# Ten more channel pairs by seven products, with three of a pair's four weight sums made ahead in place of two

## The chip, the cores and the metric

The kernel runs on one core of one Trainium2 chip, in one launch. The metric is the device time of one execution in microseconds (us), lower is better. The core's engines are TensorE (PE, with its weight loads as PEld), VectorE (DVE), ScalarE (ACT), GpSimd (POOL) and SyncE (SP, which here issues DMAs).

## The reference

A decoder trunk of two layers on 256 tokens of width 2048, all in float32. Layer 0 is a Mamba-2 mixer, layer 1 a MoBA cross-attention whose keys and values come from the stream after layer 0. Each is followed by a gated MLP with a causal convolution of width 3. Every sub-layer ends in `h = layer_norm(4**0.25 * h + f(h))`.

```
mix = mamba2_mixer(h, ...)             # ... -> y @ w_out          (4096 x 2048)
ffn = (silu(gate) * val) @ w_down      # gate, val: conv(h @ w_up) (5632 x 2048)
k_blk, v_blk, k_mean = shared_kv(h, w_kv)
mix = moba_cross_attention(h, w_q, w_o, k_blk, v_blk, k_mean)
```

What matters here are the products of the tokens with large weight matrices: `w_out`, the two `w_down`, the third of the V columns and `w_o`. All of them read each weight once.

## The kernel before, in words

A float32 product is made of three faster ones: each operand x is split into a rounded part hi (type fp32r) and a rest lo, and the product is hi*hi + hi*lo + lo*hi. The weights come in tiles `raw` of 128 x 2 x 512 (512 KB) from `in_w`, which the host has stacked in the order of use. `split` makes hi on ACT (L357) and lo on DVE (L358), up to `LA` + 1 = 4 tiles ahead of PE, in a ring of `RING` = 5 pairs of buffers; the `raw` tiles have `RAW` = 4 buffers. A tile is loaded when the one four before it has been read.

The work is one list of **steps**, a tile each; for every step the program runs what is hung before it (`pre`), its matmuls (`products`), amid which later tiles are split, and what is hung after it (`post`, by `at(i, f)`). So the order on every engine follows from the step's number, and DMAs, sums and normalizations are placed by step numbers.

Most products are ordinary. The "duos" (class `Duo`) take two neighbouring blocks of 512 columns, a and b, with the two halves of the tokens, and the channels in **pairs** of two blocks of 128. A pair is either two ordinary steps (kind `a` or `b`, twelve matmuls of 512 columns each, in `half`: L392, L393, L396) or goes **by seven products** (a form of Strassen's: seven of 128 x 128 x 512 in place of eight), as two steps `A` and `B`: two products, six matmuls, in A, and five products, fifteen matmuls, in B (`one`: L413, L414, L415). The seven need four sums of the pair's activations, and four of its four weight blocks W11, W22 (tile A), W21, W12 (tile B): W11+W12, W22+W12, W11+W12+W22 and all four. `SUMS` writes, for each matrix, the order of the steps of both its duos: `a`, `b`, and `H` for a pair by seven products whose weight sums are begun ahead.

**Weight sums ahead.** For an `H`, `plan_hoist` makes W11+W12 and W22+W12 stages earlier and keeps them in DRAM (`made`): with `away`, by a DMA that copies and one of POOL's that accumulates (L645, L648; for mamba's output and the V projection); else by loads into a tile `hoist` and a half tile `u`, one add on DVE (L661) and a store (L664). The list `starts` says at which steps; the three parts of one lie at s, s + 4 and s + 6. When the pair is due, `load` fetches for the B step W21 into `raw` (L287) and both sums into `gb` (L288; `mA` in mamba's stage), and `split_sums` adds on DVE the third (L327, which reads tile A once more) and the fourth (L328), and splits W21 (`u`, L320 and L325), the first two (L326, L329) and the last two (L330, L331).

**Activation sums.** They are made when the activations are (`make_sums`: four subtractions L597 to L600, a cast, a subtraction L607, a store to DRAM) and fetched by POOL (`fetch_sums`, L622) into eight ring slots in `hT`, each slot again when the pair that used it is done. POOL works its queue in order.

**Normalization.** The end of each duo adds its banks to the residual on DVE (`Norm.sums`, `add2`), at steps counted from the last pair by seven products; the residual tiles `r` are loaded at the start of each duo.

Of the kernel before, what the change touches and what calls it, by code (L numbers as in the profile page):

```python
# [18 lines left out]
F32 = mybir.dt.float32  # L19
F32R = mybir.dt.float32r  # L20
AF = mybir.ActivationFunctionType
OP = mybir.AluOpType
AX = mybir.AxisListType

P = 128
# [14 lines left out]
NC = 512  # L40
# [6 lines left out]
for _name, _n in (("cw", 4 * CONV), ("cb", CONV), ("nw", DI), ("fw0", 6 * DFF), ("fcb0", 2 * DFF), ("fw1", 6 * DFF),  # L47
# [10 lines left out]
SIZE = 2 * PIECE  # L58
AT = 16
RING = LA + 2  # L60
SUMS = {"mamba": ("aabbababab" + "HabHaHbHabH", "aaHaHabHaHabHaH"), "att": ("aabbHaHbHbaab", ""), "v": ("aHHaHHbHabb",),
        0: ("aabbaba" + "HaHb" * 5 + "Hbbaab", "aaHaHbHaHaHbHaHbHaHaHb"), 1: ("aabbaba" + "HaHb" * 5 + "Hbbaab", "aaHaHbHaHaHbHaHbHaHaHb")}
SLOTS = 8


# [3 lines left out]

MOST = {n: max(map(count, SUMS[k])) for n, k in ((DI, "mamba"), (D, "att"), (DFF, 0))}  # L70
INTO = {"a": ("P2", "p4"), "b": ("p3", "N22"), "A": ("P1", "p3"), "B": ("P2", "p5", "P7", "p6", "p4")}
# [3 lines left out]
def chunks():  # L75
# [71 lines left out]
def yoco_kernel(ctx: ExitStack, tc: tile.TileContext, x, lmg, lmb, lfg, lfb, x_t, columns, w, out):  # L147
    nc = tc.nc
    base = ctx.enter_context(tc.tile_pool(name="base", bufs=1))
    wts = ctx.enter_context(tc.tile_pool(name="wts", bufs=LA + 1))  # L150
    t4 = ctx.enter_context(tc.tile_pool(name="t4", bufs=4))
    psum = ctx.enter_context(tc.tile_pool(name="psum", bufs=1, space=bass.MemoryType.PSUM))
    dram = ctx.enter_context(tc.tile_pool(name="dram", bufs=1, space=bass.MemoryType.DRAM))
# [124 lines left out]
    def load():  # L278
        i = pos["load"]
        if i >= n_steps:  # L280
            return
        pos["load"] += 1
        raw_t[i] = t = wts.tile([P, 2, NC], F32, tag="raw", name="raw", bufs=RAW)
        if early(i):
            ch, s = steps[i]
            made_t[i] = y = ch.tmp()
            nc.sync.dma_start(t[:, 0], w[i][:, 0])  # L287
            nc.sync.dma_start(y, ch.sum_d[ch.items[s][1]])  # L288
            return
        for e in (slice(0, 1), slice(1, 2)) if i == 0 else (slice(0, 2),):  # L290
            nc.sync.dma_start(t[:, e], w[i][:, e])

    def early(i):
        return kind(i) == "B" and steps[i][0].items[steps[i][1]][1] in steps[i][0].sum_d
# [19 lines left out]
    def split_sums(i):  # L314

        ra, rb = raw_t.pop(i - 1), raw_t.pop(i)
        (yh, yl), (zh, zl) = (map(plain, ring_tiles()) for _ in range(2))
        wh, wl = (base.tile([P, 2, S], F32R, tag="u", name="u", bufs=2).rearrange("p k t -> p (k t)")
                  for _ in range(2))
        nc.scalar.copy(wh, rb[:, 0])  # L320
        yf, zf = (made_t.pop(i), rb) if early(i) else (steps[i][0].tmp() for _ in range(2))
        t2, t4 = (zf[:, k] for k in ((1, 0) if early(i) else (0, 1)))
        if not early(i):
            nc.vector.tensor_add(yf, ra, rb[:, 1:2, :].to_broadcast([P, 2, NC]))
        nc.vector.tensor_sub(wl, rb[:, 0], wh.bitcast(F32))  # L325
        nc.scalar.copy(yh, yf)  # L326
        nc.vector.tensor_add(t2, yf[:, 0], ra[:, 1])  # L327
        nc.vector.tensor_add(t4, t2, rb[:, 0])  # L328
        nc.vector.tensor_sub(yl, yf, yh.bitcast(F32))  # L329
        nc.scalar.copy(zh, zf)  # L330
        nc.vector.tensor_sub(zl, zf, zh.bitcast(F32))  # L331
        hi_t[i], lo_t[i] = [wh, yh, zh], [wl, yl, zl]
        load()
        load()
# [68 lines left out]
    def one(i, b, unit, h, l):  # L403
        ch, s = steps[i]
        p = ch.items[s][1]
        if isinstance(unit, int):
            u = sum_units(ch.sums, ch.slot[p])
            xh, xl = u[:, 0, unit], u[:, 1, unit]
        else:
            kk, t = unit  # L410
            xh, xl = (f(2 * p + kk)[:, t * P:(t + 1) * P] for f in (ch.x.hi, ch.x.lo))
        a, begins, ends = ch.into(b, i)
        nc.tensor.matmul(a, xh, h, start=begins, stop=False)  # L413
        nc.tensor.matmul(a, xh, l, start=False, stop=False)  # L414
        nc.tensor.matmul(a, xl, h, start=False, stop=ends)  # L415

    def duo_products(i):
        ch, s = steps[i]
        ch.use(i)
        name, p = ch.items[s]  # L420
        h, l = hi_t[i], lo_t[i]
        if name == "A":
            one(i, "P1", (0, 0), h[:, 0], l[:, 0])
            one(i, "p3", 3, h[:, 1], l[:, 1])
            run(mid, i)
            done(i)
            return splits(i)
        if name == "B":
            (wh, yh, zh), (wl, yl, zl) = h, l
            one(i, "P2", (1, 0), wh, wl)  # L430
            one(i, "p5", 0, yh[:, 0], yl[:, 0])
            one(i, "P7", 2, yh[:, 1], yl[:, 1])
            run(mid, i)
            t2, t4 = (1, 0) if early(i) else (0, 1)
            one(i, "p6", 1, zh[:, t2], zl[:, t2])
            one(i, "p4", (1, 1), zh[:, t4], zl[:, t4])
            done(i)
            return splits(i)
        side = ch.sides[name]
        ends = side.tail and i >= side.at[-side.tail]  # L440
        if side.tail and i == side.at[-side.tail]:
            side.piece = [(tp_tile() if side.tail == LAST else ch.bank[b][0])[:, :HC] for b in ("P1", "P7")]
        half(i, 0)
        if ends:
            if i < side.last:
                return splits(i)
            for q in range(2):
                for j in side.at[-side.tail:]:
                    half(j, 1, q)
                    if q:  # L450
                        done(j)
            return
        run(mid, i)
        splits(i)
        half(i, 1)
        done(i)
# [72 lines left out]
    def at(i, f, *a):  # L529
        post.setdefault(i, []).append((f, a))  # L530
# [103 lines left out]
    def plan_hoist(duo, starts, away=False):  # L634

        todo = [(du, p) for du in duo for p in du.early]
        assert len(starts) >= len(todo)
        for (du, p), s in zip(todo, starts):
            du.sum_d[p] = made = dram.tile([P, 2, NC], F32, name=f"made{du.first}_{p}")
            n = du.items.index(("A", p)) + du.first  # L640
            tiles = []
            if away:

                def copy(n=n, made=made):
                    nc.sync.dma_start(made, w[n])  # L645

                def more(n=n, made=made):
                    nc.gpsimd.dma_start(made, w[n + 1][:, 1:2].to_broadcast([P, 2, NC]), accum_op=OP.add)  # L648

                at(s, copy)  # L650
                at(s + 6, more)
                continue

            def fetch(n=n, tiles=tiles):
                tiles += [t4k("hoist"), base.tile([P, 2, S], F32, tag="u", name="u", bufs=2).rearrange("p k t -> p (k t)")]
                nc.sync.dma_start(tiles[0], w[n])
                nc.sync.dma_start(tiles[1], w[n + 1][:, 1])

            def add(tiles=tiles):
                y, b12 = tiles  # L660
                nc.vector.tensor_add(y, y, b12.unsqueeze(1).to_broadcast([P, 2, NC]))  # L661

            def store(made=made, tiles=tiles):
                nc.sync.dma_start(made, tiles[0])  # L664

            at(s, fetch)
            at(s + 4, add)
            at(s + 6, store)

# [148 lines left out]
    chX, chZ = [], []  # L818
# [19 lines left out]
    chO = duos("y", tmp_mamba)  # L838
    up0, down0 = ffn_chunks()
# [3 lines left out]
    chQ = []  # L843
# [6 lines left out]
    up1, down1 = ffn_chunks()  # L850
    n_steps = len(steps)
    for du in (chO, down0, chA, down1):
        plan_sums(du)
    plan_hoist(chO, [chX[0].first + 8 * k for k in range(12)], away=True)
    plan_hoist(down0, [up0[1][0].first + 7 * k for k in range(21)])
    plan_hoist([chW], [chV[0].first + 2 + 3 * k for k in range(5)], away=True)
    plan_hoist(chA, [chQ[0].first + 4 + 6 * k for k in range(3)])
    plan_hoist(down1, [chQ[0].first + 22 + 6 * k for k in range(4)] + [up1[1][0].first + 9 * k for k in range(17)])

    pool = {}  # L860

# [598 lines left out]
    for h in range(HEADS):  # L1460
        i, j = divmod(h, 4)
# [27 lines left out]
    def rest(h):  # L1489

        n3.center(0, h)
        n3.all_off(1, h)
        n3.store_half(1, h, eng=nc.scalar)
        n3.center(2, h)
        n3.scale(0, h)
        n3.store_half(0, h)
        n3.scale(2, h)
        n3.store_half(2, h)
        for q in range(2):
            n3.norm(3, h, slice(q * HC, (q + 1) * HC))  # L1500
# [55 lines left out]
```

## Time and profile before

| | |
|---|---|
| median of 3 runs | 2464.04 us (2461.68 to 2465.58) |
| span of the profiled execution, first to last instruction | 2461.0 us |
| PE busy | 2449.1 us, 17992 matmul records |
| DVE busy | 1897.3 us |
| ACT busy | 1390.5 us |
| POOL busy | 112.6 us |
| moved by DMA | 629.53 MB, 256 GB/s in the mean |
| mamba's output | about 483 to 650 us of the span |
| up, down of layer 0 | 682 to 1141, 1141 to 1365 us |
| K, V, Q and attention | about 1365 to 1740 us |
| up, down of layer 1 | 1767 to 2226, 2226 to 2453 us |

The profiled execution has no time of its own beside its span; the runs lie 0.7 to 4.6 us above it. A row of the timeline reads: start, duration, engine, line, operation, tiles written <- read, shapes, and in brackets the engine's idle time before it with what ended it. Matmuls overlap, so that a row's duration is longer than the distance to the next. In the rows of stretches the columns are: stretch, length, busy time (and count) of PE, PEld, DVE, ACT, POOL, the granted clock, the mean busy share of the 16 DMA engines, and GB/s.

### The profile page before, as it was taken

The page shows a single profiled execution, that of the slowest core. Times are in us where ns is not written, and L with a number is a line of the kernel's source. Part 1 is how long each engine was busy: PE and PEld are TensorE (multiplying, and loading weights), DVE is VectorE, ACT ScalarE, POOL GpSimd, SP SyncE. Part 2 cuts the span into 40 slices and gives each one's busy share as a digit, 9 for nine tenths or more (in the row PEclk, how much of TensorE's full clock was granted, in tenths as well). Part 3 has the DMA queues.
Part 4 walks back from the last instruction along what each step waited for, and adds up shares of the span by engine and source line. Part 5 has one row for each costly group of instructions (what it writes and reads, how often), then busy time and mean ns, then how long its engine had stood idle before and what let it go on. Part 6 is the DMA issues. An engine that isn't in the chain of part 4 may idle for free.

```text
span 2461.0 us, 44889 instructions
## 1 busy us (share of the span) xinstructions
PE 2449.1 (100%) x17992; PEld 2299.1 (93%) x17992; DVE 1897.3 (77%) x2533; ACT 1390.5 (57%) x1817; POOL 112.6 (5%) x147
## 2 busy tenths in 40 slices
PE   9999999999999999999999999999999999999998
PEld 9999999988899999999888889998899999998887
DVE  6768778878877777777898785768777677777997
ACT  6677677655455545545655464545555455455563
POOL 0010100100200000000000300000200000000001
PEclk9999999999999999999999999999999999999999
DMA  7677886767678787777878776768677778778775
GB/s 265 225 235 251 257 261 202 255 222 260 226 251 287 267 291 272 273 273 278 287 258 267 266 258 234 251 223 265 214 275 256 266 248 275 246 261 317 249 272 194
DMA packets 184753, 629.53 MB, mean 256 GB/s; under 512 B 20560, under 2 KB 21072, under 8 KB 184288
## 3 DMA queue, kind: packets, MB, share of 16 engines
q1 hardware_dynamic: 170032, 582.55, 68.8%
q0 software_dynamic: 14224, 43.59, 6.3%
q8 instruction: 141, 2.31, 0.4%
q14 instruction: 68, 0.56, 0.1%
q10 hardware_dynamic: 288, 0.52, 0.1%
HBM read 578.28 MB, written 65.08 MB: 261 GB/s over the span
## 4 chain that ended last, share of the span: by engine, by line
PE 98%; DVE 1%; ACT 0%; issue 0%; DMA 0%; SPq 0%; ACTq 0%
PE acc L489 62%; PE acc L392 7%; PE acc L396 7%; PE acc L393 7%; PE acc L415 3%; PE acc L413 3%; PE acc L414 3%; PE tp L415 1%; PE tp L413 1%; PE tp L414 1%; PE acc L1099 1%; PE tp L580 0%; PE tp L1108 0%; PE acc L1082 0%; PE tp L1402 0%; PE tp L1437 0%
## 5 line engine op out<-in xcount | busy, mean ns | idle before, releaser
L358 DVE TENSOR_TENSOR lo<-raw,hi 128x1024 fp32r<-128x1024 f32 (+1 forms) x808 | 973.0, 1223 | 256.8 <-ACT hi L357 254.9
L489 PE MATMUL acc<-hT,hi 128*128 128x256 f32 x8960 | 1116.1, 277 | 0.3 <-ACT hi L357 0.2
L489 PEld LDWEIGHTS acc<-hT,hi 128*128 128x128 f32 x8960 | 1061.6, 188 | 3.4 <-issue 1.2
L357 ACT CAST hi<-raw 128x1024 fp32r<-128x1024 f32 (+1 forms) x808 | 828.5, 1046 | 345.6 <-PE acc L489 138.1
L489 PE MATMUL acc<-hT,lo 128*128 128x256 f32 x4480 | 599.8, 276 | 0.0
L489 PEld LDWEIGHTS acc<-hT,lo 128*128 128x128 f32 x4480 | 550.1, 188 | 0.0
L937 DVE SCALAR_TENSOR_TENSOR v<-acc,cols,v 128x254 f32<-128x254 f32 (+1 forms) x176 | 72.7, 475 | 78.5 <-ACT v L932 78.4
L393 PE MATMUL acc<-lo,gT 128*128 128x512 f32 x334 | 129.4, 388 | 0.0
L392 PE MATMUL acc<-hi,gT 128*128 128x512 f32 x334 | 129.4, 388 | 0.0
L330 ACT CAST hi<-raw 128x1024 fp32r<-128x1024 f32 x61 | 64.3, 1055 | 87.1 <-DVE raw L328 86.5
L396 PE MATMUL acc<-hi,gT 128*128 128x512 f32 x334 | 102.5, 388 | 0.0
L932 ACT ACTIVATE v<-acc,cols 128x256 f32<-128x256 f32 x88 | 44.9, 561 | 93.8 <-PE acc L489 93.8
L622 POOL DMA_DIRECT2D hT<-sums x35 | 18.7, 539 | 1422.9 <-PE acc L489 949.4
L937 DVE SCALAR_TENSOR_TENSOR g<-acc,cols,g 128x255 f32<-128x255 f32 (+1 forms) x160 | 66.1, 475 | 19.5 <-ACT g L932 19.5
L1331 ACT CAST gT<-v 128x512 fp32r<-128x512 f32 x44 | 27.3, 621 | 93.0 <-DVE v L1330 93.0
L331 DVE TENSOR_TENSOR lo<-raw,hi 128x1024 fp32r<-128x1024 f32 x61 | 74.8, 1226 | 3.7
L393 PEld LDWEIGHTS acc<-lo,gT 128*128 128x128 f32 x334 | 62.7, 188 | 12.8
L392 PEld LDWEIGHTS acc<-hi,gT 128*128 128x128 f32 x334 | 62.7, 188 | 12.8
L396 PEld LDWEIGHTS acc<-hi,gT 128*128 128x128 f32 x334 | 62.6, 188 | 12.9
L932 ACT ACTIVATE g<-acc,cols 128x256 f32<-128x256 f32 x80 | 40.8, 560 | 42.0 <-PE acc L489 42.0
L326 ACT CAST hi<-gb 128x1024 fp32r<-128x1024 f32 x50 | 52.6, 1052 | 16.8 <-DMA gb<-made 14.6
L392 PE MATMUL acc<-hi,hT 128*128 128x512 f32 x152 | 61.9, 408 | 0.0
(332 smaller groups left out, 2946.8 us busy)
## 6 DMA issues: line engine op xcount, KB each, us to landing
raw<-in_w SPq DMA_DIRECT2D x819, 512.0 KB, 4.7
gb<-made SPq DMA_DIRECT2D x50, 512.0 KB, 5.2
hoist<-in_w SPq DMA_DIRECT2D x45, 512.0 KB, 6.4
made<-hoist SPq DMA_DIRECT2D x45, 512.0 KB, 6.2
hT<-sums POOLq DMA_DIRECT2D x35, 512.0 KB, 7.0
raw<-in_w SPq DMA_DIRECT2D x63, 256.0 KB, 3.8
sums<-st SPq DMA_DIRECT2D x31, 512.0 KB, 3.3
u<-in_w SPq DMA_DIRECT2D x45, 256.0 KB, 6.2
```

The source lines that it names most:

```text
L331: nc.vector.tensor_sub(zl, zf, zh.bitcast(F32))
L357: nc.scalar.copy(h[:, sl], t[:, sl])
L358: nc.vector.tensor_sub(l[:, sl], t[:, sl], h[:, sl].bitcast(F32))
L392: nc.tensor.matmul(a, th, h[:, kk, sl], start=begins and kk == 0, stop=False)
L393: nc.tensor.matmul(a, th, l[:, kk, sl], start=False, stop=False)
L396: nc.tensor.matmul(a, ch.x.lo(k)[:, ts], h[:, kk, sl], start=False, stop=ends and kk == 1)
L413: nc.tensor.matmul(a, xh, h, start=begins, stop=False)
L414: nc.tensor.matmul(a, xh, l, start=False, stop=False)
L415: nc.tensor.matmul(a, xl, h, start=False, stop=ends)
L489: nc.tensor.matmul(banks[j], w[:, a, n * P:(n + 1) * P], x(k0 + kk), start=k0 == 0 and j // 2 not in where[:at_n], stop=k0 + ch.per == ch. ...
L932: nc.scalar.activation(self.dst[:, self.jd + i, :], u[:, i % 2, :], AF.Identity, bias=c1(self.b, self.ia + i), scale=c1(self.at_w, w[n - 1 ...
L937: nc.vector.scalar_tensor_tensor(d, u[:, i % 2, :S - k], c1(self.at_w, w[n - 1 - k] + self.ia + i), d, op0=OP.mult, op1=OP.add)
```

## The change

1. `made` holds three sums in place of two: W11+W12, W11+W12+W22 and W22+W12. On DVE the one add of 1024 becomes three of 512; the store becomes two (512 and 256 KB). With `away`, the copy becomes two, the accumulation two of 256 KB, and a third accumulating DMA (s + 12) adds one row of sums to another, after the first two have landed.
2. For the B step `load` fetches a third piece, 256 KB of `made` into the second half of `raw`. `split_sums` adds only the fourth sum on DVE, and reads tile A no more. The last products of a B step come in another order, p6 before P7.
3. `SUMS`: mamba's output 6 and 7 pairs by seven products (before 5 and 6), each down projection 13 and 12 (before 11 and 10), often two pairs in a row.
4. The `starts` of `plan_hoist` are closer: 13 in place of 12 for mamba; 25 every 6 steps in place of 21 every 7 for down of layer 0; 4 and 21 every 7 in place of 4 and 17 every 9 for layer 1. More activation sums are made: 7 in place of 6 for mamba, 13 in place of 11 for each down projection.

```
-SUMS = {"mamba": ("aabbababab" + "HabHaHbHabH", "aaHaHabHaHabHaH"), ...
-        0: ("aabbaba" + "HaHb" * 5 + "Hbbaab", "aaHaHbHaHaHbHaHbHaHaHb"), 1: ...
+SUMS = {"mamba": ("aabbababab" + "HaHbHaHbHH", "aaHaHabHHaHbHaH"), ...
+        0: ("aabbab" + "HaHbHHaHHbHHaHbHHaHH" + "bbaab", "aaHaHHaHHbHaHHaHHaHHbaaa"), 1: ...
...
+            made = ch.sum_d[ch.items[s][1]]
             nc.sync.dma_start(t[:, 0], w[i][:, 0])
-            nc.sync.dma_start(y, ch.sum_d[ch.items[s][1]])
+            nc.sync.dma_start(y, made[:, :2])
+            nc.sync.dma_start(t[:, 1], made[:, 2])
...
-        nc.vector.tensor_add(t2, yf[:, 0], ra[:, 1])
-        nc.vector.tensor_add(t4, t2, rb[:, 0])
+        if made:
+            nc.vector.tensor_add(zf[:, 0], yf[:, 1], rb[:, 0])
+        else:
+            nc.vector.tensor_add(zf[:, 0], yf[:, 0], ra[:, 1])
+            nc.vector.tensor_add(zf[:, 1], zf[:, 0], rb[:, 0])
...
                 def copy(n=n, made=made):
-                    nc.sync.dma_start(made, w[n])
+                    nc.sync.dma_start(made[:, :2], w[n])
+                    nc.sync.dma_start(made[:, 2], w[n][:, 1])
                 def more(n=n, made=made):
-                    nc.gpsimd.dma_start(made, w[n + 1][:, 1:2].to_broadcast([P, 2, NC]), accum_op=OP.add)
+                    for k in (0, 2):
+                        nc.gpsimd.dma_start(made[:, k], w[n + 1][:, 1], accum_op=OP.add)
+                def rest(made=made):
+                    nc.gpsimd.dma_start(made[:, 1], made[:, 0], accum_op=OP.add)
                 at(s, copy)
                 at(s + 6, more)
+                at(s + 12, rest)
...
             def add(tiles=tiles):
                 y, b12 = tiles
-                nc.vector.tensor_add(y, y, b12.unsqueeze(1).to_broadcast([P, 2, NC]))
+                nc.vector.tensor_add(y[:, 0], y[:, 0], b12)
+                nc.vector.tensor_add(b12, b12, y[:, 1])
+                nc.vector.tensor_add(y[:, 1], y[:, 1], y[:, 0])
             def store(made=made, tiles=tiles):
-                nc.sync.dma_start(made, tiles[0])
+                nc.sync.dma_start(made[:, :2], tiles[0])
+                nc.sync.dma_start(made[:, 2], tiles[1])
...
-    plan_hoist(down0, [up0[1][0].first + 7 * k for k in range(21)])
+    plan_hoist(down0, [up0[1][0].first + 6 * k for k in range(25)])
```

DVE's queue at the third pair by seven products of layer 0's down projection, before: `u`, `raw`, `gb` are the pair's W21, its sums and what was made ahead, `lo` the rests, and the last two rows are an ordinary step and tile A of the next pair.

```order
L325 TENSOR_TENSOR u_13805<-raw_13749,u_13804 128x512
L327 TENSOR_TENSOR raw_13749<-gb_13750,raw_13699 128x512
L328 TENSOR_TENSOR raw_13749<-raw_13749 128x512
L329 TENSOR_TENSOR lo_13801<-gb_13750,hi_13800 128x1024
L331 TENSOR_TENSOR lo_13803<-raw_13749,hi_13802 128x1024
L358 TENSOR_TENSOR lo_13829<-raw_13753,hi_13828 128x1024
L358 TENSOR_TENSOR lo_13847<-raw_13766,hi_13846 128x1024
```

The same place now, where two pairs follow each other (L327 is the split of W21, L330 the one add, L363 the split of an ordinary tile or of tile A):

```order
L327 TENSOR_TENSOR u_13988<-raw_13927,u_13987 128x512
L330 TENSOR_TENSOR raw_13927<-gb_13928,raw_13927 128x512
L334 TENSOR_TENSOR lo_13984<-gb_13928,hi_13983 128x1024
L336 TENSOR_TENSOR lo_13986<-raw_13927,hi_13985 128x1024
L363 TENSOR_TENSOR lo_14008<-raw_13932,hi_14007 128x1024
L327 TENSOR_TENSOR u_14029<-raw_13946,u_14028 128x512
L330 TENSOR_TENSOR raw_13946<-gb_13947,raw_13946 128x512
```

One add less stands in a pair, tile A's `raw` (13699 before) is read no more in the B step, and only tile A's split stands between two B steps.

SP's queue at that place, before:

```order
L287 DMA raw_13749<-in_w 128x512
L288 DMA gb_13750<-made401_4_115 128x1024
L291 DMA raw_13753<-in_w 128x1024
L291 DMA raw_13766<-in_w 128x1024
L287 DMA raw_13814<-in_w 128x512
L288 DMA gb_13815<-made401_6_116 128x1024
```

and now:

```order
L288 DMA raw_13927<-in_w 128x512
L289 DMA gb_13928<-made401_4_119 128x1024
L290 DMA raw_13927<-made401_4_119 128x512
L293 DMA raw_13932<-in_w 128x1024
L288 DMA raw_13946<-in_w 128x512
L289 DMA gb_13947<-made401_6_120 128x1024
L290 DMA raw_13946<-made401_6_120 128x512
```

A B step's loads are three DMAs of 1024 KB together in place of two of 768, and between two of them now stands one ordinary load (tile A) where there were two.

More of the change, by code (lines that the diff above doesn't have):

```diff
@@ L60 @@
 RING = LA + 2
-SUMS = {"mamba": ("aabbababab" + "HabHaHbHabH", "aaHaHabHaHabHaH"), "att": ("aabbHaHbHbaab", ""), "v": ("aHHaHHbHabb",),
-        0: ("aabbaba" + "HaHb" * 5 + "Hbbaab", "aaHaHbHaHaHbHaHbHaHaHb"), 1: ("aabbaba" + "HaHb" * 5 + "Hbbaab", "aaHaHbHaHaHbHaHbHaHaHb")}
+SUMS = {"mamba": ("aabbababab" + "HaHbHaHbHH", "aaHaHabHHaHbHaH"), "att": ("aabbHaHbHbaab", ""), "v": ("aHHaHHbHabb",),
+        0: ("aabbab" + "HaHbHHaHHbHHaHbHHaHH" + "bbaab", "aaHaHHaHHbHaHHaHHaHHbaaa"), 1: ("aabbab" + "HaHbHHaHHbHHaHbHHaHH" + "bbaab", "aaHaHHaHHbHaHHaHHaHHbaaa")}
 SLOTS = 8
@@ L321, in split_sums @@
         yf, zf = (made_t.pop(i), rb) if early(i) else (steps[i][0].tmp() for _ in range(2))
-        t2, t4 = (zf[:, k] for k in ((1, 0) if early(i) else (0, 1)))
-        if not early(i):
+        made = early(i)
+        if not made:
             nc.vector.tensor_add(yf, ra, rb[:, 1:2, :].to_broadcast([P, 2, NC]))
@@ L431, in duo_products @@
             one(i, "p5", 0, yh[:, 0], yl[:, 0])
-            one(i, "P7", 2, yh[:, 1], yl[:, 1])
+            second, third, t4 = (("p6", 1), ("P7", 2), 0) if early(i) else (("P7", 2), ("p6", 1), 1)
+            one(i, *second, yh[:, 1], yl[:, 1])
             run(mid, i)
-            t2, t4 = (1, 0) if early(i) else (0, 1)
-            one(i, "p6", 1, zh[:, t2], zl[:, t2])
+            one(i, *third, zh[:, 1 - t4], zl[:, 1 - t4])
             one(i, "p4", (1, 1), zh[:, t4], zl[:, t4])
@@ L638, in plan_hoist @@
         for (du, p), s in zip(todo, starts):
-            du.sum_d[p] = made = dram.tile([P, 2, NC], F32, name=f"made{du.first}_{p}")
+            du.sum_d[p] = made = dram.tile([P, 3, NC], F32, name=f"made{du.first}_{p}")
             n = du.items.index(("A", p)) + du.first
@@ L853, in yoco_kernel @@
         plan_sums(du)
-    plan_hoist(chO, [chX[0].first + 8 * k for k in range(12)], away=True)
-    plan_hoist(down0, [up0[1][0].first + 7 * k for k in range(21)])
+    plan_hoist(chO, [chX[0].first + 8 * k for k in range(13)], away=True)
+    plan_hoist(down0, [up0[1][0].first + 6 * k for k in range(25)])
     plan_hoist([chW], [chV[0].first + 2 + 3 * k for k in range(5)], away=True)
     plan_hoist(chA, [chQ[0].first + 4 + 6 * k for k in range(3)])
-    plan_hoist(down1, [chQ[0].first + 22 + 6 * k for k in range(4)] + [up1[1][0].first + 9 * k for k in range(17)])
+    plan_hoist(down1, [chQ[0].first + 22 + 6 * k for k in range(4)] + [up1[1][0].first + 7 * k for k in range(21)])
     pool = {}
```

## The prediction

> **What bounds the kernel now.** I read the profile's page first, then the chain of waits, the stretches by stage, the groups by line, and last the timeline around the pairs that go by seven products. The page:
>
> ```profile
> span 2461.0 us, 44889 instructions
> ...
> PE 2449.1 (100%) x17992; PEld 2299.1 (93%) x17992; DVE 1897.3 (77%) x2533; ACT 1390.5 (57%) x1817; POOL 112.6 (5%) x147
> ...
> PE 98%; DVE 1%; ACT 0%; issue 0%; DMA 0%; SPq 0%; ACTq 0%
> ```
>
> 98% of the chain that ended last is PE. Time goes down only by taking matmuls away, as long as nothing else becomes late. What a matmul of 512 columns costs in a row of them stands in the chain of waits, where two halves of an ordinary step (six such matmuls each) follow one another:
>
> ```profile
> 631.36 0.45 PE acc L396 x2
> 632.72 0.45 PE acc L396 x2
> ```
>
> 1.36 us for six is 0.227 us each. (The groups' 388 ns is the time of one with its overlap, not its pitch.) So an ordinary step of twelve takes 2.72 us, and a pair by seven products, 21 matmuls, 4.76 us.
>
> The two stages that matter most, up and down of layer 0, in the table of stretches (columns: PE, PEld, DVE, ACT, POOL busy, clock, DMA share, GB/s):
>
> ```profile
> 682.00:1141.00 459.00, 459.00 (x4047) 458.80 (x4046) 336.66 (x458) 243.61 (x304) 3.19 (x6) 1.00 0.78 271
> 1141.00:1365.00 224.00, 224.00 (x1008) 186.24 (x1007) 196.00 (x225) 127.45 (x137) 4.94 (x10) 1.00 0.81 276
> ```
>
> PE has no gap in either. In the down stage DVE is busy 196 of 224 us: the engine that could become late is DVE, or the DMA that feeds it.
>
> **The change part by part.** *Matmuls.* A pair costs 24 matmuls as two ordinary steps and 21 by seven products. Ten more pairs (two in mamba's output, four in each down projection) remove 30: 30 x 0.227 = 6.8 us, all of it on the path. No other matmul comes or goes.
>
> *DVE at the pair.* One cycle of a pair and an ordinary step in the down stage of layer 1:
>
> ```profile
> 2369.97 0.69 DVE L325 TENSOR_TENSOR u<-raw,u 128x512 fp32r<-128x512 f32 x1
> 2370.57 0.69 DVE L327 TENSOR_TENSOR raw<-gb,raw 128x512 f32<-128x512 f32 x1
> 2371.29 0.69 DVE L328 TENSOR_TENSOR raw<-raw 128x512 f32<-128x512 f32 x1
> 2371.90 1.22 DVE L329 TENSOR_TENSOR lo<-gb,hi 128x1024 fp32r<-128x1024 f32 x1
> 2373.18 1.23 DVE L331 TENSOR_TENSOR lo<-raw,hi 128x1024 fp32r<-128x1024 f32 x1
> 2374.33 2.35 DVE L358 TENSOR_TENSOR lo<-raw,hi 128x1024 fp32r<-128x1024 f32 x2
> 2376.60 0.69 DVE L325 TENSOR_TENSOR u<-raw,u 128x512 fp32r<-128x512 f32 x1
> ```
>
> From one L325 to the next are 6.63 us of DVE against 7.48 us of PE (4.76 + 2.72). The two L358 take 2.27, so a pair alone (one L358 and the rest) is 5.50 us: longer than PE's 4.76, which is why two pairs in a row would run DVE late. The change drops one of the two adds L327, L328 (0.66 us): 4.84 us a pair. The new groups of two pairs and one ordinary step then need 2 x 4.84 + 1.14 = 10.8 us of DVE in 12.2 us of PE. Over the first stretch of a down projection, 13 pairs and 7 ordinary steps, that is 70.9 us in 80.9, 88%; before, 11 and 10 took 71.9 in 79.6, 90%. DVE is not later than before.
>
> *DVE ahead.* The prices:
>
> ```profile
> L661 DVE TENSOR_TENSOR hoist<-hoist,u 128x1024 f32<-128x1024 f32 x45 | 54.8, 1219 | 0.0
> L607 DVE TENSOR_TENSOR st<-st 128x512 fp32r<-128x512 f32 x31 | 21.5, 692 | 21.3 <-ACT st L606 21.3
> L600 DVE TENSOR_TENSOR st<-v,st 128x128 f32<-128x128 f32 x22 | 6.4, 292 | 0.8
> ```
>
> An add ahead becomes three of 512 (3 x 0.69 = 2.07 us, the row of L327) in place of one of 1.22. In the up stage of layer 0: 25 x 2.07 - 21 x 1.22 = 26 us, and two more sets of activation sums at 4 x 0.29 + 0.69 = 1.85. DVE goes from 337 to 366 of 459 us; that lies in its 122 idle us and costs nothing. If the cover were gone, each added microsecond would be on the path.
>
> *DMA at the pair.* The issues of the page:
>
> ```profile
> raw<-in_w SPq DMA_DIRECT2D x819, 512.0 KB, 4.7
> gb<-made SPq DMA_DIRECT2D x50, 512.0 KB, 5.2
> ...
> hT<-sums POOLq DMA_DIRECT2D x35, 512.0 KB, 7.0
> ...
> made<-in_w POOLq DMA_DIRECT2D x16, 512.0 KB, 10.4
> ...
> r<-hres SPq DMA_DIRECT2D x12, 512.0 KB, 7.8
> ```
>
> A pair loaded 512 + 256 + 512 KB, now 512 + 256 + 512 + 256 = 1536 KB. With 13 pairs and 8 ring slots more activation sums are fetched again (hT<-sums). The two dense places of a down projection, counted as what is consumed and fetched there: (1) from the end of the first pair to the end of the fifth in the first two columns, PE needs 4 x 4.76 + 3 x 2.72 = 27.2 us; loaded are 4 x 1536 + 3 x 512 KB, and POOL's order puts 7 fetches there: 11264 KB = 11.53 MB, 424 GB/s. (2) At the start of the second two columns, 3 pairs and 2 ordinary steps in 19.7 us, with 3 fetches and two r: 8192 KB = 8.39 MB, 425 GB/s. What the queues can give:
>
> ```profile
> 1140.00:1150.00 10.00, 10.00 (x49) 8.41 (x49) 5.84 (x9) 4.73 (x7) 0.00 (x0) 1.00 1.09 406
> ...
> 2220.00:2240.00 20.00, 20.00 (x113) 17.45 (x112) 12.73 (x17) 8.94 (x12) 2.14 (x4) 1.00 1.02 389
> ```
>
> At 389, the highest rate held over 20 us, the bytes take 29.6 and 21.6 us: 2.4 and 1.9 us late. Against that stands the lead of the last part of a pair (DVE's L331 to PE's first matmul on it), in place 1 and in place 2:
>
> ```profile
> 1218.04 1.22 DVE L331 TENSOR_TENSOR lo<-raw,hi 128x1024 fp32r<-128x1024 f32 x1
> ...
> 1259.18 1.22 DVE L331 TENSOR_TENSOR lo<-raw,hi 128x1024 fp32r<-128x1024 f32 x1
> ```
> ```profile
> 1223.25 0.39 PE L414 MATMUL tp<-lo,hT 128*128 128x512 f32 x1
> ...
> 1262.01 0.39 PE L414 MATMUL tp<-lo,hT 128*128 128x512 f32 x1
> ```
>
> 1223.25 - 1219.26 = 4.0 us; 1262.01 - 1260.40 = 1.6, and 0.7 more with the dropped add: 2.3. Both cover the lateness, narrowly. Bounds for the four places together: 0 (covered), or 17.7 us (the rival below). I take 1.1 us, four times 0.27, the size of the only wait of PE on DVE there is in mamba's output:
>
> ```profile
> 531.24 0.39 PE L392 MATMUL acc<-hi,yT 128*128 128x512 f32 x1
> 531.74 0.50 PE L393 MATMUL acc<-lo,yT 128*128 128x512 f32 x1
> ```
>
> (0.50 in place of 0.23 us.) That wait goes: DVE reaches this point with two adds less behind it, 1.3 us. What is late next is the following ordinary step, which has one ordinary step less ahead of it; I count -0.3, between -0.3 and +1.
>
> *SP and POOL.* SP issues a third load per pair and a second store per set made ahead, 0.33 to 0.43 us each in the trace, while it waits for buffers anyway: nothing. Where the sums are made by accumulating DMAs, POOL now waits for the first two to land before the third, and the V projection has the least time:
>
> ```profile
> 1420.06 1.03 POOL L648 DMA_DIRECT2D made<-in_w  x1 [5.28 <-DMA made<-in_w]
> ```
> ```profile
> 1455.80 0.38 SPq L288 DMA_DIRECT2D gb<-made  x1
> ```
>
> 1420.1 and twice 10.4 us is 1441; SP issues the load that needs it at 1455.8. Behind the waiting POOL stand only its other accumulating DMAs there. Nothing.
>
> Sum: 2461.0 - 6.8 - 0.3 + 1.1 = 2455.0 us of span. The median of the runs, 2464.04, lies 3.0 above the profiled span, and the lowest 0.7; with 3.0 I forecast 2458.0.
>
> **The rivals.** *The DMA does not keep up (slower).* The same stretches by share also read the other way: if a share of 1.0 is all there is, this row gives 263 / 0.82 = 321 GB/s.
>
> ```profile
> 1290.00:1300.00 10.00, 10.00 (x46) 8.28 (x45) 9.88 (x11) 6.67 (x8) 0.00 (x0) 1.00 0.82 263
> ```
>
> Then place 1 takes 35.9 us, 8.7 late less 4.0 of lead, and place 2 26.1, 6.4 late less 2.3: 8.8 us in each down projection, 17.7 in all, 2464.0 - 7.1 + 17.7 = 2474.6. The gain is gone below about 350 GB/s (3.6 us in each), slower by over 0.2% below about 337. For it: loads landed later where the rate was high. Against: the rows with 1.09 and 1.02. Chance 0.08.
>
> *The DMA gives 349 in the dense places (no change).* That is the rate at which it runs where loads and accumulating DMAs crowd:
>
> ```profile
> 1400.00:1420.00 20.00, 20.00 (x179) 20.00 (x178) 15.05 (x22) 11.31 (x14) 2.07 (x2) 1.00 1.06 349
> ```
>
> Place 1 then loses 33.0 - 27.2 - 4.0 = 1.8 us and place 2 24.0 - 19.7 - 2.3 = 2.0, 7.7 in all: 2464.0 - 7.1 + 7.7 = 2464.6. For it: that share, too, is above 1. Against: 389 over as long a stretch, with as many fetches of sums in it. Chance 0.16. [...]
>
> *The V projection is late (little change).* The row just shown is its stage, and its ordinary steps have this lead:
>
> ```profile
> 1400.04 1.05 ACT L357 CAST hi<-raw 128x1024 fp32r<-128x1024 f32 x1
> ```
> ```profile
> 1406.11 1.07 PE L489 MATMUL acc<-hT,hi 128*128 128x256 f32 x8
> ```
>
> Five pairs add 256 KB of copy and 256 KB of accumulation each, 2.6 MB, 7.5 us at 349 GB/s; the cast leads PE by 5.0. At worst 2.5 us are lost: 2464.0 - 7.1 + 2.5 + 1.1 = 2460.5. Chance 0.11.
>
> That the change doesn't remove the matmuls is no rival: PE's instructions are 30 fewer.
>
> **How the numbers follow.** Forecast 0.64; the V projection 0.11 and the DMA at 349 GB/s 0.16, both "same"; the slow DMA 0.08; 0.01 for the unforeseen, slower. A measurement of this kernel can tell about 0.2%, 4.9 us, from no change: faster is below 2459.1, slower above 2469.0. So 0.64, 0.27, 0.09. The range runs from the full gain with nothing lost (2456.9), less the 1.5 us by which runs scatter, to the time of the rival at 349 GB/s, which it just takes in: 2455.4 to 2464.7. It leaves out the slow DMA and little else.
>
> **What would show it.** Right: PE's 512-column matmuls 30 fewer; each down stage shorter by 2.7 us (4 x 0.68) and mamba's output by 1.4 to 1.7; no wait of PE above 0.3 us; DVE's pair at 4.84 us; the dense places at 380 to 420 GB/s. Wrong: the rate stuck near 320 to 350 in them while DVE idles for ACT casts that wait for raw, and PE waits for lo or hi there; or PE gaps in the V projection.

## The result, and the profile after

The changed kernel takes 2490.03 us, median of 4 runs (2484.29 to 2498.72), the kernel before on the same chips 2463.39 (2461.68 to 2465.58): ratio 1.0113, interval 1.0096 to 1.013. It is slower by 1.1% where 0.2% faster was forecast, and its runs lie 14 us apart where those of before lie 4. The profiled execution is the slowest of the four (2498.72 us, span 2497.0), so the tables below account for 36.0 us, where the medians differ by 26.6. Its page:

```profile
span 2497.0 us, 45484 instructions
...
PE 2468.6 (99%) x17962; PEld 2312.4 (93%) x17962; DVE 1943.6 (78%) x2641; ACT 1413.3 (57%) x1842; POOL 145.3 (6%) x194
...
PE 34%; DMA 4%; DVE 4%; ACT 2%; issue 1%; SPq 0%; POOL 0%; ACTq 0%; DVEq 0%
```

PE has its 30 matmuls fewer and is busy 19.5 us longer, in a span 36.0 us longer. From PE's rows in the timeline, first to last matmul of each stage, in us:

| stage | before | after | difference |
|---|---|---|---|
| up to mamba's output | 485.56 | 483.81 | -1.75 |
| mamba's output | 169.60 | 167.80 | -1.80 |
| its end (normalization) | 27.80 | 29.21 | +1.41 |
| up, layer 0 | 457.76 | 480.14 | **+22.38** |
| down, layer 0 | 224.14 | 223.68 | -0.46 |
| its end | 27.78 | 29.04 | +1.26 |
| K and V | 83.70 | 88.09 | +4.39 |
| Q and attention, with its output | 263.40 | 269.89 | +6.49 |
| its end | 27.75 | 27.80 | +0.05 |
| up, layer 1 | 457.76 | 460.97 | +3.21 |
| down, layer 1 | 225.89 | 226.71 | +0.82 |

Mamba's output is shorter by about what was forecast; the down stages, forecast 2.7 us shorter each, are 0.46 shorter and 0.82 longer. The time was lost mostly where no matmul was touched: in the up stages, where the sums are made ahead, in the V projection and in the attention.

**Up, layer 0.** PE's rows in the timeline, an ordinary step of 24 matmuls of 256 columns early in the stage and around the second of its two waits:

```profile
719.70 1.98 PE L494 MATMUL acc<-hT,hi 128*128 128x256 f32 x16
...
722.42 1.98 PE L494 MATMUL acc<-hT,hi 128*128 128x256 f32 x16
...
818.62 3.60 PE L494 MATMUL acc<-hT,hi 128*128 128x256 f32 x16 [2.94 <-ACT hi L362]
...
823.01 2.06 PE L494 MATMUL acc<-hT,hi 128*128 128x256 f32 x16
...
825.85 2.06 PE L494 MATMUL acc<-hT,hi 128*128 128x256 f32 x16
```

The step took 722.42 - 719.70 = 2.72 us, and takes 825.85 - 823.01 = 2.84 after the waits: 118.3 ns a matmul in place of 113.3. It keeps this longer pitch from the first wait, at 770 us, to the end of the stage at 1161: 391 us x 5.0 / 118.3 = 16.5 us. The two waits themselves are 1.15 and 2.94 us, and the granted clock is 0.50 for 3.4 us behind the longer one (columns as in the prediction; the third row is a part of the first two):

```profile
815.00:820.00 5.00, 2.06 (x12) 1.85 (x11) 4.05 (x11) 3.91 (x6) 0.00 (x0) 0.85 0.99 356
820.00:825.00 5.00, 5.00 (x37) 5.00 (x36) 4.97 (x6) 2.32 (x4) 0.00 (x0) 0.81 0.90 312
...
818.50:821.80 3.30, 3.18 (x15) 3.18 (x16) 3.30 (x6) 3.30 (x6) 0.00 (x0) 0.50 1.01 373
```

What PE waited for is a cast of ACT at 817.53 us. A cast of a tile before it had waited 4.86 us for its load, and between the two ACT also made casts for two sets of activation sums (810.27 and 816.09 us), so this one wait alone doesn't say which of the two it is due to. SP's rows ahead of the late load show what was issued before it:

```profile
805.01 1.05 ACT L362 CAST hi<-raw 128x1024 fp32r<-128x1024 f32 x1 [4.86 <-DMA raw<-in_w]
```
```profile
793.74 0.42 SPq L677 DMA_DIRECT2D made<-hoist  x1
794.21 0.42 SPq L678 DMA_DIRECT2D made<-u  x1
794.68 0.97 SPq L667 DMA_DIRECT2D hoist<-in_w  x1
795.69 1.78 SPq L668 DMA_DIRECT2D u<-in_w  x1
797.58 10.10 SPq L293 DMA_DIRECT2D raw<-in_w  x5
```

The sums of one pair are stored at s + 6, and with one begun every six steps that is the step at which the next pair's tiles are loaded: 512 + 256 + 512 + 256 = 1536 KB in one row ahead of the next `raw`. Before, a store was 512 KB and a step lay between.

**Attention.** The chain of waits in one head:

```profile
1574.10 7.06 DMA made<-u
1581.18 0.59 ACT u L1458
1581.80 0.70 DVE aT L1459
```

The third sum is stored from the half tile `u`, of which there are two. Before, `u` was free after DVE's add at s + 4; now it is held until the store at s + 6 has landed, and ACT's copy of a head's output needs the same buffer.

**The V projection.** The stretch of its accumulating DMAs, and the load on the chain that ended before PE's first wait there:

```profile
1410.00:1460.00 50.00, 48.57 (x406) 47.30 (x405) 28.92 (x43) 20.57 (x24) 12.41 (x15) 1.00 1.07 330
```
```profile
1439.91 11.96 DMA raw<-in_w
```

**The down projections.** The first dense place in the rates, and PE's wait in it:

```profile
1185.00:1205.00 20.00, 19.44 (x86) 15.75 (x86) 13.11 (x15) 10.16 (x12) 2.13 (x4) 1.00 1.08 405
```
```profile
1202.78 0.50 PE L398 MATMUL acc<-lo,gT 128*128 128x512 f32 x1 [0.56 <-DVE lo L363]
```

DVE's pair is what was forecast. Between two pairs in a row:

```profile
1210.00 0.68 DVE L327 TENSOR_TENSOR u<-raw,u 128x512 fp32r<-128x512 f32 x1
1210.72 0.69 DVE L330 TENSOR_TENSOR raw<-gb,raw 128x512 f32<-128x512 f32 x1
1211.33 1.22 DVE L334 TENSOR_TENSOR lo<-gb,hi 128x1024 fp32r<-128x1024 f32 x1
1212.57 1.23 DVE L336 TENSOR_TENSOR lo<-raw,hi 128x1024 fp32r<-128x1024 f32 x1
1213.71 2.35 DVE L363 TENSOR_TENSOR lo<-raw,hi 128x1024 fp32r<-128x1024 f32 x2
```

1213.71 - 1210.00 = 3.71 us, and 1.13 for tile A: 4.84. The lead of the last part of a pair (end of DVE's L336 to PE's first matmul on it) at the third and the fourth pair of this place:

```profile
1190.16 1.23 DVE L336 TENSOR_TENSOR lo<-raw,hi 128x1024 fp32r<-128x1024 f32 x1
...
1198.06 1.23 DVE L336 TENSOR_TENSOR lo<-raw,hi 128x1024 fp32r<-128x1024 f32 x1 [0.53 <-ACT hi L335]
```
```profile
1195.93 0.39 PE L419 MATMUL acc<-lo,hT 128*128 128x512 f32 x1
...
1200.69 0.39 PE L419 MATMUL acc<-lo,hT 128*128 128x512 f32 x1
```

It is 1195.93 - 1191.39 = 4.5 us at the third and 1200.69 - 1199.29 = 1.4 at the fourth; the ordinary tile behind the fourth is the one that PE waited for.

### The profile page after: what moved, and what is told of

Its sections match the earlier page's. It is cut to its first block, busy times and chain, and to the rows that moved or that the text cites. A ratio compares the mean times of both kernels' runs of the same rounds, so it can differ in the third digit from the quotient of the medians.

```text
span 2497.0 us, 45484 instructions
## 1 busy us (share of the span) xinstructions
PE 2468.6 (99%) x17962; PEld 2312.4 (93%) x17962; DVE 1943.6 (78%) x2641; ACT 1413.3 (57%) x1842; POOL 145.3 (6%) x194
## 5 line engine op out<-in xcount | busy, mean ns | idle before, releaser
L363 DVE TENSOR_TENSOR lo<-raw,hi 128x1024 fp32r<-128x1024 f32 (+1 forms) x798 | 960.0, 1223 | 255.6 <-ACT hi L362 251.9
L494 PE MATMUL acc<-hT,hi 128*128 128x256 f32 x8960 | 1130.5, 279 | 6.8 <-ACT hi L362 6.8
L494 PEld LDWEIGHTS acc<-hT,hi 128*128 128x128 f32 x8960 | 1075.1, 188 | 10.4 <-ACT hi L362 8.1
L398 PE MATMUL acc<-lo,gT 128*128 128x512 f32 (+1 forms) x270 | 104.8, 388 | 0.6 <-DVE lo L363 0.6
L397 PE MATMUL acc<-hi,gT 128*128 128x512 f32 (+1 forms) x270 | 104.6, 388 | 0.0
L336 DVE TENSOR_TENSOR lo<-raw,hi 128x1024 fp32r<-128x1024 f32 x71 | 86.9, 1224 | 6.0 <-ACT hi L335 2.1
L401 PE MATMUL acc<-hi,gT 128*128 128x512 f32 (+1 forms) x270 | 82.7, 387 | 0.0
L334 DVE TENSOR_TENSOR lo<-gb,hi 128x1024 fp32r<-128x1024 f32 x58 | 70.8, 1221 | 4.1 <-ACT hi L328 3.7
L322 ACT CAST u<-raw 128x512 fp32r<-128x512 f32 x71 | 44.1, 621 | 49.2 <-PE acc L419 29.2
L327 DVE TENSOR_TENSOR u<-raw,u 128x512 fp32r<-128x512 f32 x71 | 48.8, 687 | 20.1 <-ACT u L322 19.4
L611 ACT CAST st<-st 128x512 fp32r<-128x512 f32 x36 | 22.4, 621 | 69.6 <-DVE st L605 67.9
```

What stands on the lines that cost most here:

```text
L363: nc.vector.tensor_sub(l[:, sl], t[:, sl], h[:, sl].bitcast(F32))
L397: nc.tensor.matmul(a, th, h[:, kk, sl], start=begins and kk == 0, stop=False)
L398: nc.tensor.matmul(a, th, l[:, kk, sl], start=False, stop=False)
L401: nc.tensor.matmul(a, ch.x.lo(k)[:, ts], h[:, kk, sl], start=False, stop=ends and kk == 1)
L494: nc.tensor.matmul(banks[j], w[:, a, n * P:(n + 1) * P], x(k0 + kk), start=k0 == 0 and j // 2 not in where[:at_n], stop=k0 + ch.per == ch. ...
```

## The experiments

Theories at the start, on the up stages, where most was lost. **A**: thirteen sets of activation sums need two sets in the second and third block of an up stage, as there were before only in the first; two sets in a row leave ACT and DVE one tile to split in about 10 us (758.6 to 768.8 in the trace), and both waits of PE, at 770 and 818 us, fall there. **B**: the transfers of the sums ahead make raw tiles land late. **C**: it takes both. A stage is named here with its time in the profiled execution.

**e1_sums13.** The kernel before with two sets of activation sums more.

```
+MOST[DFF] = 13
```

> The kernel before with thirteen sets of activation sums made in each up stage in place of eleven (the two added ones are stored and never fetched); nothing else is changed. Theory A, two sets in one block keep ACT and DVE from splitting for about 10 us and this alone empties the lead: PE waits at the second and third block of an up stage, 1 to 3 us each, and its pitch on 256 columns goes from 113 to 118 ns after it; 2468 to 2490 us. Theory B, the heavier traffic of the sums made ahead delays the raw tiles: no gap of PE in the up stages, within 0.2% of before. Theory C, it takes both: the smallest lead at these blocks falls to 1 to 2.5 us without a gap, within 0.2% of before.

2463.36 us (2461.24 to 2477.72), ratio 1.0006 (0.9996 to 1.0017); both up stages 457.76 us, no wait. A falls.

**e2_spread.** The changed kernel, the second set four steps later.

```
-            if 2 * j + half in made_of:
-                make_sums(...)
...
+            for half, step in ((0, 3), (1, 8 if 2 * j in made_of else 4)):
+                if 2 * j + half in made_of:
+                    at(cv.end + step, gated_sums, j, half)
```

> The changed kernel with the second of two sets of activation sums of one block made four steps later, so that splits come between them. Theories A and C: the up stages run without a gap at 113 ns, 458 us each, and the median falls by 15 to 25 us to 2464 to 2472, with a smaller scatter; what is lost in the attention, the V projection, the ends of the stages and the down projections stays. Theory B: the gaps in the up stages stay, 2484 to 2499 us as the changed kernel.

2485.98 us (2482.44 to 2491.14), ratio 1.0096 (1.0083 to 1.0109). Up of layer 1 is clean, 457.76 us; up of layer 0 takes 467.00 with six waits of 0.4 to 1.6 us, at 816, 861, 946, 951, 1080 and 1085 us, most of them in blocks with one set. For layer 0, C falls as well; for layer 1, where sums are begun every seven steps, it fits.

**e3_pairs.** Points 3 and 4 of the change without 1 and 2: the new `SUMS` and `starts` in the code of before, two sums ahead.

> The ten more pairs, with the new places of the sums made ahead, but two sums ahead as before (third and fourth added on DVE when due). Theory A: up stages lose as in the changed kernel (5 to 25 us), attention and V projection lose nothing; 2465 to 2485. Theory B: traffic is nearly that of before, the up stages are clean, 2456 to 2464. Either way the down stages show whether DVE at 5.50 us a pair keeps up where two pairs follow each other.

2470.32 us (2469.31 to 2483.85), ratio 1.004 (1.0025 to 1.0056). Attention 263.40 and K and V 83.69 as before; up of layer 0 459.01 with one wait of 0.84 us, up of layer 1 clean. The ends after mamba's output and after the first down projection take 29.67 and 29.58, so that they come with the new pairs and without the third sum. The median lies in A's range and not in B's, but the time went to these ends and to the down stages, not to the up stages. The down stages take 223.76 and 228.82 us: with DVE at 5.50 us a pair the second one is 5.7 us above 225.89 - 2.72, so that the third sum does serve its purpose there.

**e4_third.** Points 1 and 2 without 3 and 4: the third sum ahead, with pairs and spacing of before.

> The third sum made ahead, with the pairs and places of before. The attention's loss is put down to the half tile u, which is now held until its store has landed, and not to the new pairs: it should be here in full, 5 to 7 us at three heads, and the V projection's 3 to 5 us too. Theories A and C: the up stages are clean, 458 us each; in all 2470 to 2476 us. Theory B: the up stages have gaps here too, above 2476 us.

2470.84 us (2469.68 to 2488.06), ratio 1.0053 (1.0031 to 1.0076). Both up stages 457.76. K and V take 88.29, +4.6: the V projection's loss belongs to the third sum. The attention takes 265.96, +2.6: less than the 5 to 7 expected, as its two waits for the store of `u` are 2.7 us together here and 6.0 with the change.

**e5_every6.** The same, the sums of the first down projection every six steps.

```
-    plan_hoist(down0, [up0[1][0].first + 7 * k for k in range(21)])
+    plan_hoist(down0, [up0[1][0].first + 6 * k for k in range(21)])
```

> The kernel with only the third sum ahead (pairs and activation sums of before), its sums for the down projection of layer 0 begun every six steps in place of every seven. Only the spacing differs from the run before it without the new pairs, 2470.8 us. Theory B, now made precise (every six steps the store of one pair's sums and the loads of the next are issued at the same step, 1536 KB in a row; DVE's add then waits for its loads and raw tiles land late): DVE waits 15 us or more for u in the up stage of layer 0, where it waited 3.1 us at every seven, PE has gaps there, the stage takes 459 to 475 us in place of 457.8, and the median is 2472 to 2488. Theory C (it takes the second set of activation sums too): the stage stays at 457.8 us and the median within 2 us of 2470.8.

2482.37 us (2472.70 to 2488.16), ratio 1.0067 (1.0047 to 1.0087). By the ratios that isn't clear of e4_third (1.0053, 1.0031 to 1.0076): two of its six runs take 2472.70 us, the others 2478 to 2488, and two of e4_third's seven lie as high. The stage of the profiled execution (2487.41 us) shows it: up of layer 0 takes 473.90 us in place of 457.76. PE waits once:

```profile
811.73 2.04 PE L494 MATMUL acc<-hT,hi 128*128 128x256 f32 x16
...
816.09 2.16 PE L494 MATMUL acc<-hT,hi 128*128 128x256 f32 x16 [1.42 <-ACT hi L362]
...
819.03 2.06 PE L494 MATMUL acc<-hT,hi 128*128 128x256 f32 x16
...
821.87 2.06 PE L494 MATMUL acc<-hT,hi 128*128 128x256 f32 x16
```

Steps take 2.84 us from there to the end of the stage. So 1.42 us of waiting cost 16.1. DVE's wait for `u` in the waits of the stage, at every seven steps (e4_third) and at every six:

```profile
DVE hoist L672 <- DMA u<-in_w: 3.1, 3, 1.4
```
```profile
DVE hoist L672 <- DMA u<-in_w: 19.1, 11, 2.9
```

With no pair and no set of activation sums added, the spacing is enough for the wait: B. It takes the third sum too: in e3_pairs, every six steps with two sums, the row is 1280 KB, and the stage lost 1.25 us.

**e6_att.** The changed kernel with another tile for the seven pairs made ahead in the attention.

```
-                tiles += [t4k("hoist"), base.tile([P, 2, S], F32, tag="u", ...)]
+                tiles += [t4k("hoist"), tmp_att()[:, 0] if du is chA[0] or s < up1[0][0].first and du in down1 else base.tile([P, 2, S], F32, tag="u", ...)]
```

> The changed kernel with another tile (one of the three gb of the attention's own pool) in place of the half tile u for the seven pairs whose sums are made in Q and attention. If ACT's copy to u, which waits for the store of the third sum to land, makes the attention late: K to attention's end falls from 269.9 to 263.4 to 265 us, and the median by 5 to 6 us to 2478 to 2486 (with the changed kernel's scatter). Rival, the 0.85 us that the three adds take longer on DVE ahead of the softmax: it stays at 268 to 270 us.

Q and attention take 263.69 us in place of 269.89, and ACT's copy waits no more; the three adds, which are still there, leave 0.3. The cause is shown. The median, 2487.60 us (2483.57 to 2512.11), ratio 1.0118 (1.0087 to 1.0148), doesn't show it: the profiled execution, the slowest, has up stages of 481.42 and 478.44 us, the second after one wait of 2.54 us at 1887.

**e7_hold.** The kernel before with six holds on DVE.

```
+    def hold():
+        t = t4k("hold")
+        for _ in range(18):
+            nc.vector.tensor_add(t[:, 0]..., hT[:, 0:2, 0]..., hT[:, 0:2, 1]...)
+    for up in (up0, up1):
+        for j in (2, 5, 8):
+            at(up[j][1].first + 2, hold)
```

> The kernel before with six deliberate holds: 18 additions of 512 columns on DVE, 11 to 12 us in a row, in the third, sixth and ninth block of each up stage, so that PE runs out of split tiles there once. If a wait can put PE's row of matmuls into the slower pitch: after some of the six the pitch is 118 ns in place of 113 up to the next wait or the end of the stage, and the runs scatter by 10 us or more, between 2475 and 2510. If a wait costs only its own length and a moment of lower clock: the pitch is 113 ns after each, the time is 2464 and six times 1 to 5 us, with a scatter below 5 us.

2497.16 us (2494.83 to 2504.55), ratio 1.0144 (1.013 to 1.0157). PE's rows at two of the holds:

```profile
1888.28 1.98 PE L489 MATMUL acc<-hT,hi 128*128 128x256 f32 x16
...
1890.99 1.98 PE L489 MATMUL acc<-hT,hi 128*128 128x256 f32 x16
1893.99 1.21 PE L489 MATMUL acc<-hT,lo 128*128 128x256 f32 x8 [1.02 <-DVE lo L358]
1895.05 2.06 PE L489 MATMUL acc<-hT,hi 128*128 128x256 f32 x16
...
1897.88 2.06 PE L489 MATMUL acc<-hT,hi 128*128 128x256 f32 x16
```
```profile
2025.68 2.06 PE L489 MATMUL acc<-hT,hi 128*128 128x256 f32 x16
...
2032.19 1.20 PE L489 MATMUL acc<-hT,lo 128*128 128x256 f32 x8 [1.61 <-DVE lo L358]
2033.23 1.98 PE L489 MATMUL acc<-hT,hi 128*128 128x256 f32 x16
...
2035.95 1.98 PE L489 MATMUL acc<-hT,hi 128*128 128x256 f32 x16
```

A wait of 1.02 us is followed by steps of 2.83 us, and the next wait, 138 us later, by steps of 2.72 again. The three holds of layer 0 and the last one are followed by the short pitch. So a wait can switch the pitch, in a kernel without any of the change's transfers, and need not.

**e8_add5.** The changed kernel, the adds ahead one step later.

```
-            at(s + 4, add)
+            at(s + 5, add)
```

> The changed kernel with the adds of the sums ahead one step later (five after the load in place of four). If DVE's wait for u (21.6 us in all in the up stage of layer 0, 14 times) is what starves PE there: that wait falls below 5 us, the up stage is free of gaps or nearly, 458 to 462 us, and the median falls to 2466 to 2474. If it is the raw tiles that land late in any case: the gaps stay, and the median is 2480 or more.

2505.25 us (2504.18 to 2507.98), ratio 1.0173 (1.016 to 1.0186): worse. DVE no longer waits for `u` at all, but ACT's wait for raw tiles in that stage doubles (the changed kernel's row first):

```profile
ACT hi L362 <- DMA raw<-in_w: 61.9, 37, 4.9
```
```profile
ACT hi L362 <- DMA raw<-in_w: 127.5, 73, 5.7
```

So DVE's wait was a symptom; the raw tiles are what is late. The stage takes 484.81 us. Why they land still later here was not separated.

**e9_apart.** e2_spread with the transfers of the first down projection's sums apart; the same bytes every six steps.

```
-            at(s, fetch)
-            at(s + 4, add)
-            at(s + 6, store)
+            for step, f in zip((0, 1, 5, 8, 9) if apart else (0, 0, 4, 6, 6), (fetch, fetch2, add, store, store2)):
+                at(s + step, f)
```

> The changed kernel with the second set of activation sums four steps later (as in the run with that edit alone, 2485.98 us, up stage of layer 0 467.0 us), and besides with the transfers of the sums ahead for layer 0's down projection spread over the steps: the two loads at s and s + 1, the adds at s + 5, the two stores at s + 8 and s + 9, so that at most 512 KB of them are issued at a step in place of 1536. Bytes and spacing are the same. If it is the 1536 KB in a row that delay the raw tiles: the up stage is free of gaps, 457.8 to 459.5 us, and the median is 2470 to 2476. Rival, the bytes as such (about 300 GB/s wanted in this stage): gaps or the slower pitch stay, 464 us or more, and the median is 2478 or more.

2473.42 us (2471.52 to 2476.56), ratio 1.004 (1.0026 to 1.0053). Up of layer 0 takes 457.76 us, without a wait, at a mean of 299 GB/s:

```profile
683.00:1139.00 456.00, 456.00 (x4025) 456.00 (x4025) 364.04 (x522) 246.07 (x305) 2.66 (x5) 1.00 0.85 299
```

The bytes fit: it was the 1536 KB in one row. The adds are a step later here too, which alone doesn't help (e8_add5); whether taking apart only the stores or only the loads would do was not tried, nor the edit without that of e2_spread.

**e10_all.** The same, with the attention's other tile and two sums ahead for the V projection.

```
+            if not two(i):
                 nc.sync.dma_start(t[:, 1], made[:, 2])
...
+        if two(i):
+            nc.vector.tensor_add(zf[:, 1], yf[:, 0], ra[:, 1])
+            nc.vector.tensor_add(zf[:, 0], zf[:, 1], rb[:, 0])
```

> The run with the transfers apart, and besides the tile gb in place of u for the seven pairs made ahead in the attention, and only two sums ahead for the V projection's five pairs (third and fourth added on DVE, as in the kernel before). If the parts found so far are the whole: attention 263.4 to 264, K and V 83.7, up stages 457.8 each; what is left are the ends of two stages (1.3 us each) and the waits in the down projections (2 us each) against 6.8 us of matmuls, 2459 to 2464 us, from the same as before to 0.2% faster. If the up stage of layer 0 is not clean, it falls in the same way as the run with the transfers apart, less 10 us.

2464.26 us (2460.91 to 2467.14, 11 runs), ratio 1.0002 (0.9993 to 1.0011): the same as before. K and V 83.70, Q and attention 263.68, both up stages 457.76; the median lies just above the 2459 to 2464 us that was expected. Of the 26.6 us between the medians, 16.6 went with the edits of e9_apart and 9.2 with these. PE's waits in the profiled execution, the fastest of the eleven (span 2459.2 us), those at the start of the kernel left out:

```profile
...
PE tp L592 <- DVE r L799: 1.4, 2, 0.9
PE acc L405 <- DVE hT L370: 1.2, 2, 0.8
PE tp L426 <- DVE lo L341: 0.7, 1, 0.7
```

These are the two ends, the last tiles of the last down projection, and the second dense place of the first. The down stages take 223.54 and 226.17 us and keep 0.3 us of their 5.4.

**e11_23** and **e12_mamba.** The same with fewer pairs in the down projections: 12 and 11, and 11 and 10 as before.

```
-"aabbab" + "HaHbHHaHHbHHaHbHHaHH" + "bbaab", "aaHaHHaHHbHaHHaHHaHHbaaa"
+"aabbab" + "HaHbHaHHbHaHbHHaHbHH" + "bbaab", "aaHaHbHaHHbHaHbHaHHaHb"
```

> The run with all remedies, with 12 and 11 pairs by seven products in each down projection in place of 13 and 12 (21 before), two pairs in a row only where that can't be avoided. If it is the density of the pairs that made the down projections wait (their DMA at over 400 GB/s for 20 us), they now keep their gain: 2 x 0.68 = 1.4 us each, 222.8 and 224.5 us, against 223.5 and 226.2 with 25 pairs; 2457 to 2463 us. Rival, that the sums' third piece costs this at any density: both stay at or above 224.1 and 225.9, 2460 to 2465.

> The run with all remedies, with the 21 pairs of before in each down projection at the spacing of before; the two pairs more in mamba's output stay. Mamba's output 167.8 us as with the change (169.6 before), the end of that stage 28 to 29.5 us (27.8 before), the down projections 224.1 and 225.9 if three pieces a pair cost nothing where no two pairs follow each other; 2460 to 2464 us, not to be told from before.

With 23 pairs 2462.22 us (2458.89 to 2464.97), ratio 0.9997 (0.9988 to 1.0006): the first down stage has its 222.78, the second takes 226.10, its gain lost in a wait of 0.75 us for the last tiles and smaller ones; the end between them takes 29.59. With 21 pairs 2463.39 us (2461.49 to 2466.10), ratio 1.000 (0.9991 to 1.0009): 224.14 and 226.36, mamba's output 167.80 and its end 28.99. None of them can be told from the kernel before.

## Why the prediction was wrong, point by point

- **Matmuls.** Right: 30 fewer, and mamba's output 1.80 us shorter where 1.4 to 1.7 was named, 1.36 for its six matmuls and the rest for the wait there, which went.
- **DVE at the pair.** Right, 4.84 us, and e3_pairs shows what two pairs in a row cost without it.
- **DVE ahead, "lies in its 122 idle us and costs nothing".** This is the step that failed. DVE did have the time (366 of 480 us busy). But a pair's sums made ahead are also 768 KB loaded and 768 stored (before, 512 stored), and I counted bytes only where pairs are used. Every six steps with a store at s + 6 puts both into one row of SP's queue. The term put at nothing measured 22.4 us in up of layer 0; e5_every6 has the loss without pairs or activation sums (473.90 us), and e9_apart has neither the row nor the loss (457.76). "SP issues a third load and a second store while it waits for buffers anyway: nothing" failed in the same place: behind them stand the raw tiles.
- **No term for what follows a wait.** Of the 22.4 us, 4.1 are waits and 16.5 the longer pitch behind them; the remaining 1.8 fit the 3.4 us at a clock of 0.50. My rivals priced waits at their own length. The start of the kernel had the same effect the other way: PE went at 118 ns up to 57 us before and at 113 after, which is the 1.75 us gained there. That is luck: e2_spread, with all of the change, starts at 118.
- **Nothing on how long a tile is held.** The attention's 6.5 us come from `u` (e6_att: 6.2 of them). The diff shows it: the store reads `tiles[1]`.
- **The V projection.** The rival had the mechanism, bytes on a full DMA, and was priced 2.5 us at worst; 4.4 were lost. The estimate took 349 GB/s; with accumulating DMAs from DRAM to DRAM among them the rate was 330 over 50 us, at a share of 1.07. e4_third and e10_all show that the loss is the third sum's; that it is its bytes rests on this share and on the load of 11.96 us. POOL's waits ("nothing") do not stand in the chain ahead of PE's first wait there, a load does.
- **DMA at the pair.** 1.1 us was forecast; 2.3 and 3.5 were lost (223.68 and 226.71 against 221.42 and 223.17). Other executions with these pairs and sums lost 1.5 to 3.2 and 1.4 to 3.1 (222.9 to 224.6 and 224.6 to 226.3 us, e2_spread, e6_att, e8_add5, e9_apart, e10_all), so the sizes are rough. The rate was above my 389, 405 GB/s over 20 us, so the rivals with 321 and 349 are out there. The lead of 4.0 us was there too, 4.5 at the third pair, and was used up by the ordinary tile behind the fourth. The mis-sized term is the lateness: about 5 us by then, where 2.4 was summed for the whole place. Why was not separated; five of the place's seven fetches of activation sums were issued in its first 8 us (POOL's rows at 1181.89 and 1189.37), and my sum had spread them over 27.2. At 23 pairs the first down stage keeps its gain (e11_23). The last tiles of the second wait in every version with more pairs; what makes them late was not separated.
- **The ends.** Not in the sum: 1.4 and 1.3 us. Before, DVE's last row of the normalization that PE's transposes need ended at 1364.61 us (L769, 1363.83 + 0.78) and they began at 1364.70: 0.09 us of slack. That later raw tiles in the last steps took more than that is argued, not shown; e1_sums13 and e7_hold, with the pairs of before, also took 28.42 and 28.45 us after mamba's output, so part of the 1.4 is not the change's.

The sum of the profiled execution: -6.8 (matmuls) - 0.4 (mamba's wait) - 1.8 (start) + 22.4 + 3.2 (up) + 6.5 + 4.4 + 2.7 (ends) + 2.3 + 3.5 (down) = 36.0 us. The forecast had the first two and 1.1.

## What to carry to other kernels

Work that is moved ahead is paid in bytes where it is moved to: count them there, and look at which step its stores meet the next one's loads in a queue that feeds the bound engine. For every tile that a new instruction reads, ask until when it is now held and who else takes a buffer of that tag. A stage without one wait is worth more than its idle time says, since here a first wait of 1.15 us was followed by the longer pitch for 391 us.

## What the runs showed of the hardware that was not expected

PE's row of 256-column matmuls, each with its own weight load, ran at one of two pitches in these traces, 113.3 or 118.3 ns, at a granted clock of 1.00 in both (the changed kernel, 690 to 769 and 822 to 1160 us). It kept the short one through whole stages (457.76 us) and the long one for about 380 us without a wait (e6_att, from 1892 us to the end of the stage). It changed at waits, where another kind of matmul came in (the kernel before, from the long to the short one around its 512-column matmuls at 51.92 to 55.61 us), and once, in e7_hold at 2191 us, without a wait in the list. Of 29 waits that met the short pitch in the up stages of the seven profiled executions that have any there, 8 were followed by the long one; of what decides it nothing was found. The single runs that lie 14 to 17 us above their median (2477.72, 2483.85, 2485.57, 2488.06 us) fit it, but weren't profiled.

After the wait of 2.94 us the granted clock was 0.50 from 818.5 to 821.9 us, and 16 matmuls took 3.44 us in place of 1.89. A wait of 2.54 us in e6_att had the same behind it (0.50 from 1887.7 to 1891.0), one of 2.49 us in e8_add5 had not (1.00 from 773 to 778).
